# Keys and values of the attention branch: norm, rotation, high/low splits and transposes moved from the first pass to the convolution pass

## The chip, the cores and the metric

The kernel runs on one core of one Trainium2 chip. The metric is the device time of one execution in microseconds (us); lower is better. TensorE is written PE here (PEld for its weight loads), VectorE is DVE, ScalarE is ACT, GpSimd is POOL, and SP is the queue that issues most of the DMAs.

## The reference, cut to what matters

One layer of a hybrid backbone: 2048 latent tokens and 256 context tokens of width 1024 are normalised and modulated, projected by one matrix, mixed by two branches, and projected back. The change touches keys and values of branch B only:

```python
h = _rmsnorm(x, norm_w) * (1.0 + scale[:, None]) + shift[:, None]
hc = _rmsnorm(ctx, norm_w) * (1.0 + scale_c) + shift_c
qkv_c, beta_c, decay_c, kb_c, vb_c = _split_cols(hc @ w_state, STATE_SIZES)
kb_c = _rmsnorm(kb_c.reshape(b, lc, ATT_KV_HEADS, ATT_HD), k_norm_w)
qkv, beta_r, decay_r, kb, vb = _split_cols(h @ w_state, STATE_SIZES)
qa, ka, va, g, bt = _gdn_inputs(qkv, beta_r, decay_r, conv_w, a_log, dt_bias)   # 5-tap convolutions
kb = _axial_rope(_rmsnorm(kb.reshape(b, l, ATT_KV_HEADS, ATT_HD), k_norm_w), pos_row, pos_col)
vb = vb.reshape(b, l, ATT_KV_HEADS, ATT_HD)
ob = _latent_attention(qb, kb, vb, kb_c, vb_c, sink)
```

There are two key/value heads of 64, so per token 128 key numbers and 128 value numbers. Keys get a root-mean-square norm per head and, for latent tokens, a rotation by position; values stay as projected.

## The kernel before

Tokens are cut into 18 chunks of 128 (2 of context, then 16 latent). fp32 operands of the large products are split into a high and a low part (fp32r), so each product is three matmuls.

**First pass.** Chunks go in pairs: one context pair, then eight latent pairs (the loop over `gi`). For each pair: `load_x` (L280) brings two tiles `xt` of 512 KB; `norm_x` takes the mean square (half on ACT, L289, half on DVE, L292), the power -0.5 on POOL (`rsq`, L72), and scales `xt` (L295); `make_h` transposes 16 blocks on PE (L336), modulates on ACT (L337), and splits into `hh` on POOL (L339) and `hl` on DVE (L340); `tm_dense` multiplies 272 columns of `w_in` (decay and beta, keys, values) in 48 matmuls per pair (L366 to L368) into the PSUM tile `tmps`. Then `state_pair` reads `tmps`: it copies 16 columns to `bg` (L423), splits values into `vst` on ACT and DVE (L425, L426) and writes them to DRAM (`Vsp`), squares keys (L427), reduces them (L430, L431), takes the power on POOL (L72, tile `ssn`), scales (L435), rotates (L450 and L454 on DVE, L453 on POOL, with the table `cw` loaded and multiplied by the norm's weight at L443, L444), splits into `kh` (L456 to L458), transposes 4 blocks per chunk on PE (L464, tile `kt`), copies them out of PSUM (L465) and writes them to DRAM (`Ksp`). All of this works from one buffer each (`VB, SB, KB = 1, 1, 1`); `xt` has four.

**Convolution pass (`qkv`).** Twelve column tiles of 128 of the other branch's queries, keys and values are computed over five segments (one of 256 context tokens, four of 512 latent tokens) by `fm_dense` (L524 to L526, tile `lps`), copied out by ACT (L634), convolved (`conv`: L561 on ACT, four times L563 on DVE, L564 on ACT, L565 on DVE), and finished (`finish`): transposes (L595, tile `zt`), for keys also products `gps` (L604) times a decay loaded as `dtl` (L606) and another transposition (L618). The order of column tiles is `ORDER = [8, 9, 10, 11, 4, 5, 6, 7]`: four for values ("v part"), then four for keys ("k part"); the four for queries come later beside attention's own queries ("q part", `q_pass`). After each segment the loop calls `next(beside)`, which runs one step of a generator with other work; before the change this generator is `all_decays`, with 18 steps. There are 8 x 5 = 40 such calls in the v and k parts.

Later stages (gates, triangular solves, the recurrent scan, attention, projections) read `Ksp` and `Vsp` only from 1329 us on.

**What sets the order.** Each engine works through its instructions in a fixed order. This order is made when the kernel is built: the framework goes through the program by priority (the program's order) and places each instruction by a timeline that it estimates, so that work written later can be put ahead of work that waits. Tiles come from pools with a number of buffers; a tile that has no free buffer waits for the release of an older one. DMAs on SP are issued in order too: one that waits holds up those behind it.

Of the kernel before, what the change touches and what calls it, by code (L numbers as in the profile page):

```python
# [25 lines left out]
VB, SB, KB = 1, 1, 1  # L26
# [14 lines left out]
def _hybrid(ctx, tc, nc, V, S, G, T, ins, out, dbg, upto):  # L41
# [48 lines left out]
    Vsp = dscr("Vsp", [NC, 128, 2, 128])  # L90
    Qsp = dscr("Qsp", [NB, 128, 8, 128])
# [160 lines left out]
    if True:  # L252
        px_ = tc.tile_pool(name="p0x", bufs=4, reuse_waits="tile")
# [133 lines left out]
        wn = norm_w(pa, "k_norm_w")  # L387

# [29 lines left out]
        def state_pair(c, pss):  # L418

            vst = pa.tile([128, 2, 2, 2, 64], F32R, name="vst", bufs=VB)  # L420
            sq = pa.tile([128, 4, 64], F32, name="sq", bufs=SB)
            for i, ps in enumerate(pss):
                S.copy(bg[:, c + i], ps[:, 0:16])  # L423
                pv = ps[:, 144:272].rearrange("p (h d) -> p h d", d=64)
                S.copy(vst[:, i, :, 0], pv)  # L425
                V.tensor_tensor(vst[:, i, :, 1], pv, f32(vst[:, i, :, 0]), op=ALU.subtract)  # L426
                S.activation(sq[:, i * 2:i * 2 + 2], ps[:, 16:144].rearrange("p (h d) -> p h d", d=64), AF.Square)  # L427
            dma(Vsp[c:c + 2].rearrange("c p h x -> p c (h x)"), f32(vst.rearrange("p c h x d -> p c (h x d)")))
            ss = pa.tile([128, 4], F32, name="ssn")
            V.tensor_reduce(ss, sq, axis=AX.X, op=ALU.add)  # L430
            V.tensor_scalar(ss, ss, 1.0 / 64, EPS, op0=ALU.mult, op1=ALU.add)  # L431
            rsq(ss, ss)
            xn = pa.tile([128, 4, 64], F32, name="xn", bufs=SB)
            for i, ps in enumerate(pss):
                V.tensor_tensor(xn[:, i * 2:i * 2 + 2], ps[:, 16:144].rearrange("p (h d) -> p h d", d=64),  # L435
                                ss[:, i * 2:i * 2 + 2].unsqueeze(2).to_broadcast([128, 2, 64]), op=ALU.mult)
            y = xn
            if c < NCB:
                V.tensor_tensor(y, xn, wn[:, 0].unsqueeze(1).to_broadcast([128, 4, 64]), op=ALU.mult)
            else:  # L440
                cw = pa.tile([128, 2, 2, 64], F32, name="cw")
                with tc.issue_after(wm_dma.ins):
                    dma(cw, ins["k_rope"][(c - NCB) * 128:(c - NCB + 2) * 128].rearrange("(c p) x d -> p c x d", p=128))  # L443
                G.tensor_tensor(cw, cw, wn.unsqueeze(1).to_broadcast([128, 2, 2, 64]), op=ALU.mult)  # L444
# [15 lines left out]
            for i in range(2):  # L460
                kt = psum("hps" if c == NC - 2 and i else "kt", [128, 2, 2, 128], F32R, name="kt")
                for h in range(2):
                    for x in range(2):
                        T.transpose(kt[:, h, x], kh[:, i * 2 + h, x].rearrange("p r d -> p (r d)"), identr)  # L464
# [915 lines left out]
```

## Time and profile before

| | us |
|---|---|
| median of 3 runs | 2011.59 |
| lowest and highest run | 2009.54, 2018.15 |
| the profiled execution | 2010.84 |
| its span in the trace | 2009.1 |
| PE busy | 1936.4 (96% of the span) |
| DVE busy | 1407.5 (70%) |
| ACT busy | 786.1 (39%) |
| POOL busy | 654.0 (33%) |

The profiled execution took 0.75 us less than the median. Its time minus its span is 1.7 us. "Busy" of PE counts a matmul from its start to its modelled end, and successive matmuls overlap, so PE can be called busy while it delivers less than it could; therefore the distance from the start of one matmul to the next is read from the timeline, too. Times in the trace are counted from the span's start.

### The profile page before, as it was taken

Reading aid. Unit: us, or ns where it says so; the run is one execution under the profiler, and the core shown is the slowest. Engines: PE = TensorE matmul, PEld = TensorE weight load, DVE = VectorE, ACT = ScalarE, POOL = GpSimd, SP = SyncE. Lnnn points to the kernel's source line nnn. Section 1 sums busy time; section 2 is a strip of 40 time slices with the busy share of each in tenths; the row PEclk is TensorE's granted clock in tenths of the full one; section 3 lists DMA queues with packets and bytes.
Section 4 is the critical chain, followed back from the end, with each engine's and each line's share of the span. In section 5 each row is a group of like instructions: output and inputs, shape, how many; then the busy total and the mean of one; then the engine's idle time right before and its main releaser. Section 6 shows DMA issues by size and latency. Waiting matters only on the chain. (4 is left out here: it accounts for less than half of the span.)

```text
span 2009.1 us, 32070 instructions
## 1 busy us (share of the span) xinstructions
PE 1936.4 (96%) x11043; PEld 1625.3 (81%) x11043; DVE 1407.5 (70%) x2780; ACT 786.1 (39%) x1975; POOL 654.0 (33%) x751
## 2 busy tenths in 40 slices
PE   6999999989999999999999999999999999999999
PEld 3888888778998778877888888888778887878887
DVE  7979766667776899999777776536687878643322
ACT  5755545544443322211222233225665656531100
POOL 1752111225443212004222234323555444432221
PEclk8999999999999999999999999999999999999999
DMA  7552326764546633537887777674455555365542
GB/s 260 166 137 83 102 87 157 184 162 147 167 142 164 184 115 110 142 100 215 230 245 221 235 207 217 195 218 129 150 184 166 184 162 178 90 195 181 183 141 94
DMA packets 375511, 333.11 MB, mean 166 GB/s; under 512 B 83833, under 2 KB 299185, under 8 KB 374709
## 3 DMA queue, kind: packets, MB, share of 16 engines
q1 hardware_dynamic: 347924, 288.59, 49.7%
q10 hardware_dynamic: 27424, 42.48, 5.9%
q8 instruction: 87, 1.43, 0.3%
q14 instruction: 76, 0.61, 0.1%
HBM read 220.28 MB, written 109.13 MB: 164 GB/s over the span
## 5 line engine op out<-in xcount | busy, mean ns | idle before, releaser
L524 PE MATMUL rps<-hh,wh 128*128 128x512 f32 x768 | 308.4, 402 | 5.4 <-DVE rt L818 4.2
L526 PE MATMUL rps<-hh,wl 128*128 128x512 f32 x768 | 308.3, 402 | 0.0
L525 PE MATMUL rps<-hl,wh 128*128 128x512 f32 x768 | 306.4, 399 | 0.0
L563 DVE SCALAR_TENSOR_TENSOR cacc<-y,cw,cacc 128x512 f32<-128x512 f32 (+1 forms) x224 | 162.8, 748 | 22.4 <-ACT cacc L561 18.2
L524 PEld LDWEIGHTS rps<-hh,wh 128*128 128x128 f32 x768 | 145.0, 189 | 40.1 <-DVE rt L818 4.8
L524 PE MATMUL lps<-hh,wh 128*128 128x512 f32 (+1 forms) x448 | 171.4, 383 | 0.2 <-ACT y L634 0.2
L526 PE MATMUL lps<-hh,wl 128*128 128x512 f32 (+1 forms) x448 | 171.5, 383 | 0.0
L526 PEld LDWEIGHTS rps<-hh,wl 128*128 128x128 f32 x768 | 145.0, 189 | 32.6
L525 PE MATMUL lps<-hl,wh 128*128 128x512 f32 (+1 forms) x448 | 171.2, 382 | 0.0
L525 PEld LDWEIGHTS rps<-hl,wh 128*128 128x128 f32 x768 | 145.0, 189 | 32.4
L945 DVE TENSOR_TENSOR pl<-pt,ph 128x512 fp32r<-128x512 f32 x156 | 105.5, 686 | 42.1 <-ACT ph L943 41.2
L943 ACT CAST ph<-pt 128x512 fp32r<-128x512 f32 x156 | 90.1, 584 | 110.2 <-PE pt L941 77.2
L917 DVE CUSTOM_DVE_ANT_0 pr<-sc,band,sk 128x640 f32<-128x640 f32 (+1 forms) x128 | 106.8, 862 | 32.7 <-PE sc L913 16.9
L816 ACT ACTIVATE rt<-rps 128x512 f32<-128x512 f32 x96 | 57.2, 595 | 176.0 <-PE rps L526 159.1
L749 DVE TENSOR_TENSOR N<-N,btmp 128x62 f32<-128x62 f32 (+30 forms) x124 | 117.7, 949 | 3.0
L747 DVE TENSOR_TENSOR btmp<-N 128x62 f32<-128x62 f32 (+30 forms) x124 | 116.1, 936 | 3.1
L927 POOL TENSOR_SCALAR pr<-pr,sm 128x640 f32<-128x640 f32 (+1 forms) x128 | 99.2, 794 | 56.1 <-DVE sm L925 38.3
L1229 PE MATMUL pps<-yh,wph 128*128 128x512 f32 x256 | 105.2, 415 | 7.2 <-ACT yh L1211 5.0
L919 ACT ACTIVATE pr<-pr,sm 128x640 f32<-128x640 f32 (+1 forms) x128 | 104.0, 815 | 19.8 <-DVE sm L917 19.8
L246 DVE TENSOR_TENSOR wl<-wr,wh 128x512 fp32r<-128x512 f32 x120 | 91.6, 776 | 23.9 <-POOL wh L245 21.3
L245 POOL TENSOR_SCALAR wh<-wr 128x512 fp32r<-128x512 f32 x72 | 48.1, 683 | 167.1 <-PE lps L525 67.6
L1230 PE MATMUL pps<-yl,wph 128*128 128x512 f32 x256 | 101.7, 397 | 0.0
(301 smaller groups left out, 4922.8 us busy)
## 6 DMA issues: line engine op xcount, KB each, us to landing
wr<-in_w_in_dram SPq DMA_DIRECT2D x120, 256.0 KB
kw<-Ksp SPq DMA_DIRECT2D x28, 384.0 KB
x<-vsp SPq DMA_DIRECT2D x36, 256.0 KB
k<-ksp SPq DMA_DIRECT2D x34, 256.0 KB
kT<-kTsp SPq DMA_DIRECT2D x34, 256.0 KB
wm<-in_w_mod_dram SPq DMA_DIRECT2D x16, 512.0 KB
xt<-in_x_dram SPq DMA_DIRECT2D x16, 512.0 KB
dtl<-Dsp SPq DMA_DIRECT2D x32, 256.0 KB
```

The source lines that it names most:

```text
L524: T.matmul(ps, lhsT=wh[:, k], rhs=xh[:, k], start=k == 0, stop=False)
L525: T.matmul(ps, lhsT=wh[:, k], rhs=xl[:, k], start=False, stop=False)
L526: T.matmul(ps, lhsT=wl[:, k], rhs=xh[:, k], start=False, stop=k == kt - 1)
L563: V.scalar_tensor_tensor(a, y[:, t:t + n], cw[:, m, t:t + 1], a, op0=ALU.mult, op1=ALU.add)
L747: V.tensor_tensor(tv, A[:, m + 1:, m].unsqueeze(2).to_broadcast([h1 + n, r, m]), A[:, m, 0:m].unsqueeze(1).to_broadcast([h1 + n, r, m]), o ...
L749: V.tensor_tensor(A[:, m + 1:, 0:m], A[:, m + 1:, 0:m], tv, op=ALU.add)
L917: V.tensor_tensor_reduce(s_, ps[:, o:768], band[:, b0:b0 + W + 256], -0.125, sk[:, 1, hd:hd + 1], ALU.add, ALU.min, sm[:, h, 1:2])
L919: S.activation(s_, s_, AF.Exp, scale=-1.0, bias=sm[:, h, 1:2], accum_out=sm[:, h, 2:3])
L927: G.tensor_scalar(p[:, h, :W + 256], p[:, h, :W + 256], sm[:, h, 3:4], 1.0, op0=ALU.mult, op1=ALU.mult)
L945: V.tensor_tensor(pl, pt, f32(ph), op=ALU.subtract)
L1229: T.matmul(ps, lhsT=wh[:, k, ms], rhs=hs[k], start=k == 0, stop=False)
L1230: T.matmul(ps, lhsT=wh[:, k, ms], rhs=ls[k], start=False, stop=False)
```

## The change

`state_pair` now only copies `bg` and the 256 raw key and value columns out of PSUM (two ACT copies per chunk) and writes them as they are to a new DRAM tensor `Rsp`, 256 KB per pair. A new generator `key_pair` loads them again and does what `state_pair` did, with the same arithmetic: split of values, norm, rotation, split of keys, transposes, and writes of `Vsp` and `Ksp`. It takes its tiles from a pool `keys` with one buffer each, which lies where the decays' pool lay, and from the convolution pass's tags `st`, `o` and (in PSUM) `zt`, which it shares with `finish` and the decays. It is chained behind the 18 steps of the decays, and yields twice per pair: 18 + 18 = 36 steps of the 40 calls. `xt` gets six buffers instead of four.

```diff
-VB, SB, KB = 1, 1, 1
...
+    Rsp = dscr("Rsp", [NC, 128, 256])
...
-        px_ = tc.tile_pool(name="p0x", bufs=4, reuse_waits="tile")
+        px_ = tc.tile_pool(name="p0x", bufs=6, reuse_waits="tile")
...
         def state_pair(c, pss):
+            raw = pa.tile([128, 2, 256], F32, name="raw")
             for i, ps in enumerate(pss):
                 S.copy(bg[:, c + i], ps[:, 0:16])
...
+                S.copy(raw[:, i], ps[:, 16:272])
+            dma(Rsp[c:c + 2].rearrange("c p x -> p c x"), raw)
+
+        def key_pair(pool, c, wn):
+
+            raw = pool.tile([128, 2, 256], F32, name="raw")
+            dma(raw, Rsp[c:c + 2].rearrange("c p x -> p c x"))
+            cw = pool.tile([128, 2, 2, 64], F32, name="kcw")
+            if c >= NCB:
+                dma(cw, ins["k_rope"][(c - NCB) * 128:(c - NCB + 2) * 128].rearrange("(c p) x d -> p c x d", p=128))
+                G.tensor_tensor(cw, cw, wn.unsqueeze(1).to_broadcast([128, 2, 2, 64]), op=ALU.mult)
+            pv = raw[:, :, 128:256].rearrange("p c (h d) -> p c h d", d=64)
+            vst = pb.tile([128, 2, 2, 2, 64], F32R, name="vst", tag="st")
+            S.copy(vst[:, :, :, 0], pv)
+            V.tensor_tensor(vst[:, :, :, 1], pv, f32(vst[:, :, :, 0]), op=ALU.subtract)
+            dma(Vsp[c:c + 2].rearrange("c p h x -> p c (h x)"), f32(vst.rearrange("p c h x d -> p c (h x d)")))
...
+            S.activation(sq, xk, AF.Square)
...
+            V.tensor_reduce(ss, sq.rearrange("p c h d -> p (c h) d"), axis=AX.X, op=ALU.add)
+            V.tensor_scalar(ss, ss, 1.0 / 64, EPS, op0=ALU.mult, op1=ALU.add)
             rsq(ss, ss)
+            V.tensor_tensor(xk, xk, ss.rearrange("p (c h) -> p c h", c=2).unsqueeze(3).to_broadcast([128, 2, 2, 64]),
+                            op=ALU.mult)
+            yield
...
+                        V.tensor_tensor(halves(t2)[:, :, :, b], halves(xk)[:, :, :, 1 - b],
+                                        sw[:, :, b].unsqueeze(1).to_broadcast([128, 2, 2, 16]), op=ALU.mult)
+                G.tensor_tensor(xk, xk, cw[:, :, 0].unsqueeze(2).to_broadcast([128, 2, 2, 64]), op=ALU.mult)
+                V.tensor_tensor(xk, xk, t2, op=ALU.add)
             for i in range(2):
+                kh = pb.tile([128, 2, 2, 2, 64], F32R, name="kh", tag="st")
+                S.copy(kh[:, :, 0], xk[:, i].unsqueeze(2).to_broadcast([128, 2, 2, 64]))
+                V.tensor_tensor(kh[:, :, 1, 0], xk[:, i], f32(kh[:, :, 0, 0]), op=ALU.subtract)
+                V.tensor_copy(kh[:, :, 1, 1], f32(kh[:, :, 1, 0]))
+                kt = psum("zt", [128, 2, 2, 128], F32R, name="kt")
                 for h in range(2):
                     for x in range(2):
+                        T.transpose(kt[:, h, x], kh[:, h, x].rearrange("p r d -> p (r d)"), identr)
+                ks = pb.tile([128, 2, 2, 128], F32, name="ks", tag="o")
+                S.copy(ks, f32(kt))
+                dma(Ksp[:, :, :, (c + i) * 128:(c + i + 1) * 128].rearrange("h x p t -> p h x t"), ks)
+            yield
...
-    def all_decays():
+    def beside_kv():
...
+        dc_.__exit__(None, None, None)
+        with tc.tile_pool(name="keys", bufs=1, side="right", reuse_waits="tile") as kp:
+            wn = norm_w(kp, "k_norm_w")
+            for c in range(0, NC, 2):
+                for _ in key_pair(kp, c, wn):
+                    yield
...
-    qkv(ORDER, None, first_w, all_decays())
+    jobs = beside_kv()
+    qkv(ORDER, None, first_w, jobs)
+    for _ in jobs:
+        pass
     scalars2(pb)
```

More of the change, by code (lines that the diff above doesn't have):

```diff
@@ L385, in norm_w @@
             return wn
-        wn = norm_w(pa, "k_norm_w")
         def qk_norm_rope(pool, bufs, ps, nh, c, wn):
@@ L428, in state_pair @@
-            dma(Vsp[c:c + 2].rearrange("c p h x -> p c (h x)"), f32(vst.rearrange("p c h x d -> p c (h x d)")))
-            ss = pa.tile([128, 4], F32, name="ssn")
-            V.tensor_reduce(ss, sq, axis=AX.X, op=ALU.add)
+                S.copy(raw[:, i], ps[:, 16:272])
[11 more added lines that the diff above has]
+            V.tensor_tensor(vst[:, :, :, 1], pv, f32(vst[:, :, :, 0]), op=ALU.subtract)
+            dma(Vsp[c:c + 2].rearrange("c p h x -> p c (h x)"), f32(vst.rearrange("p c h x d -> p c (h x d)")))
+            xk = raw[:, :, 0:128].rearrange("p c (h d) -> p c h d", d=64)
+            sq = pool.tile([128, 2, 2, 64], F32, name="sq", tag="sq")
+            S.activation(sq, xk, AF.Square)
+            ss = pool.tile([128, 4], F32, name="ssn")
+            V.tensor_reduce(ss, sq.rearrange("p c h d -> p (c h) d"), axis=AX.X, op=ALU.add)
@@ L456, in state_pair @@
-            S.copy(kh[:, :, 0], y.unsqueeze(2).to_broadcast([128, 4, 2, 64]))
-            V.tensor_tensor(kh[:, :, 1, 0], y, f32(kh[:, :, 0, 0]), op=ALU.subtract)
-            V.tensor_copy(kh[:, :, 1, 1], f32(kh[:, :, 1, 0]))
-            ks = pa.tile([128, 2, 2, 2, 128], F32, name="ks", bufs=KB)
-            for i in range(2):
-                kt = psum("hps" if c == NC - 2 and i else "kt", [128, 2, 2, 128], F32R, name="kt")
+                        V.tensor_tensor(halves(t2)[:, :, :, b], halves(xk)[:, :, :, 1 - b],
+                                        sw[:, :, b].unsqueeze(1).to_broadcast([128, 2, 2, 16]), op=ALU.mult)
@@ L462, in state_pair @@
                 for h in range(2):
                     for x in range(2):
-                        T.transpose(kt[:, h, x], kh[:, i * 2 + h, x].rearrange("p r d -> p (r d)"), identr)
-                S.copy(ks[:, :, :, i], f32(kt))
-            for h in range(2):
-                dma(Ksp[h, :, :, c * 128:(c + 2) * 128].rearrange("x p t -> p x t"), ks[:, h].rearrange("p x c t -> p x (c t)"))
+                        T.transpose(kt[:, h, x], kh[:, h, x].rearrange("p r d -> p (r d)"), identr)
+                ks = pb.tile([128, 2, 2, 128], F32, name="ks", tag="o")
```

36 lines of the change are left out of this document (7 added, 29 removed).

## The prediction

> **What bounds the kernel now.** First the page:
>
> ```profile
> span 2009.1 us, 32070 instructions
> PE 1936.4 (96%) x11043; PEld 1625.3 (81%) x11043; DVE 1407.5 (70%) x2780; ACT 786.1 (39%) x1975; POOL 654.0 (33%) x751
> ```
>
> PE is the bound, so the change can gain only where PE falls short of its rate, and pays wherever PE gets work it cannot overlap. Next the windows over the stages that the change touches: start, first pass, v part, k part, start of the q part, rest of the q part (windows overlap; PEclk is the granted clock):
>
> ```profile
> core 0: us, PE busy (x) PEld busy (x) DVE busy (x) ACT busy (x) POOL busy (x), PEclk, DMA share, GB/s
> 0.00:50.00 50.00, 34.69 (x135) 16.99 (x136) 35.09 (x62) 29.70 (x47) 8.46 (x16) 0.83 0.74 261
> 50.00:140.00 90.00, 82.11 (x617) 76.84 (x616) 76.59 (x195) 60.26 (x168) 57.92 (x69) 0.96 0.48 153
> 160.00:200.00 40.00, 39.34 (x192) 32.25 (x191) 37.73 (x66) 24.51 (x59) 11.81 (x11) 1.00 0.25 79
> 253.00:375.00 122.00, 121.05 (x662) 102.00 (x661) 76.42 (x147) 62.00 (x183) 15.99 (x17) 1.00 0.50 131
> 350.00:460.00 110.00, 97.75 (x595) 83.66 (x594) 74.83 (x154) 54.76 (x182) 29.25 (x33) 0.97 0.67 173
> 475.00:600.00 125.00, 125.00 (x876) 114.38 (x876) 91.03 (x214) 55.56 (x168) 62.31 (x73) 1.00 0.48 144
> ```
>
> In the first pass PE idles 7.9 of 90 us and DVE is 85% busy; in the k part PE is full and DVE has 45.6 us free. PE loses more in the first pass than its idle time says. ACT's copies of `bg`, in the timeline, mark the ends of the context pair, the first latent pair and the last:
>
> ```profile
> 54.62 0.17 ACT L423 COPY bg<-tmps 128x16 f32<-128x16 f32 x1
> ...
> 63.33 0.17 ACT L423 COPY bg<-tmps 128x16 f32<-128x16 f32 x1
> ...
> 137.70 0.17 ACT L423 COPY bg<-tmps 128x16 f32<-128x16 f32 x1
> ```
>
> Eight latent pairs take 83.1 us, 10.4 each; the first took 8.7. What PE needs, by its timeline:
>
> ```profile
> 50.54 0.49 PE L336 MATMUL hps<-ident,xt 128*128 128x128 f32 x3
> 50.78 0.50 PE L366 MATMUL tmps<-wh,hh 128*128 128x272 f32 x2
> 51.12 0.49 PE L336 MATMUL hps<-ident,xt 128*128 128x128 f32 x3
> 51.37 0.37 PE L367 MATMUL tmps<-wh,hl 128*128 128x272 f32 x1
> 51.58 0.28 PE L368 MATMUL tmps<-wl,hh 128*128 128x272 f32 x1
> ...
> 52.57 0.28 PE L367 MATMUL tmps<-wh,hl 128*128 128x272 f32 x1
> ```
>
> Eight starts from 51.58 to 52.57 give 0.124 us per product. From 50.54 to 51.58 there are three products (0.37) and six transposes, 0.11 each. A pair's 48 products and 16 transposes cost 6.0 + 1.8 = 7.8 us. That is the floor without key transposes.
>
> **The change, part by part.** *Off the first pass.* DVE's rows of `state_pair`, 50 to 140 us, and PE's key transposes:
>
> ```profile
> L450 DVE TENSOR_TENSOR t<-xn,cw 128x64 f32<-128x64 f32 x28 | 6.0, 262 | 0.0
> L454 DVE TENSOR_TENSOR xn<-xn,t 128x256 f32<-128x256 f32 x7 | 5.4, 772 | 2.2 <-POOL xn L453 2.2
> L426 DVE TENSOR_TENSOR vst<-tmps,vst 128x128 fp32r<-128x128 f32 x18 | 5.0, 281 | 1.4 <-ACT vst L425 1.4
> L457 DVE TENSOR_TENSOR kh<-xn,kh 128x256 fp32r<-128x256 f32 x8 | 4.4, 548 | 0.9 <-ACT kh L456 0.8
> L435 DVE TENSOR_TENSOR xn<-tmps,ssn 128x128 f32<-128x128 f32 x16 | 3.9, 285 | 4.2 <-POOL ssn L72 4.1
> L430 DVE TENSOR_REDUCE ssn<-sq 128x4 f32<-128x256 f32 x8 | 3.3, 412 | 0.6 <-ACT sq L427 0.5
> L458 DVE CAST kh<-kh 128x256 fp32r<-128x256 f32 x8 | 2.6, 321 | 0.0
> L431 DVE TENSOR_SCALAR ssn<-ssn 128x4 f32<-128x4 f32 x8 | 1.7, 217 | 0.1
> L464 PE MATMUL kt<-identr,kh 128*128 128x128 f32 x57 | 8.6, 253 | 2.9 <-DVE kh L458 2.0 <-ACT ks L465 0.9
> ```
>
> DVE's eight rows sum to 32.3 us for about eight pairs, 4.0 each; without them DVE needs some 45 of the window's 90, and PE with 7.8 per pair is left the slowest. In DVE's queue of the first pass the middle of a pair was:
>
> ```order
> L435 TENSOR_TENSOR xn<-tmps,ssn 128x128 x2
> L292 SCALAR_TENSOR_TENSOR junk_1100,ss<-xt 128x512
> L450 TENSOR_TENSOR t_731<-xn,cw 128x4x16 x2
> L295 TENSOR_SCALAR xt<-xt,rstd 128x1024
> L450 TENSOR_TENSOR t_731<-xn,cw 128x4x16 x2
> ```
>
> and now, at the same place, is (L340 is the low part `hl`, which PE waits for; `h` is what ACT modulated):
>
> ```order
> L340 TENSOR_TENSOR hl_152<-h_836,hh_151 128x2x256
> L340 TENSOR_TENSOR hl_152<-h_847,hh_151 128x2x256
> L340 TENSOR_TENSOR hl_152<-h_858,hh_151 128x2x256
> L292 SCALAR_TENSOR_TENSOR junk_1175,ss<-xt 128x512
> L340 TENSOR_TENSOR hl_152<-h_947,hh_151 128x2x256
> ```
>
> Nothing but the next pairs' norms stands between the low parts now; the waits for POOL (4.1 us before L435, 2.2 before L454) are gone from ahead of PE's operands. What is late next is PE itself, or ACT, which modulates; ACT's own part gets shorter too (two copies per chunk remain). The pace lies between 7.8 (floor) and 10.4 (nothing gained); nearest is the first latent pair's 8.7, which still had DVE's key work beside it. I take 8.2: 8 x (10.4 - 8.2) = **-17.6 us** (-20.8 at the floor, -13.6 at 8.7).
>
> *Start.* SP issued before:
>
> ```order
> L280 DMA xt<-in_x_dram 128x1024 x2
> L443 DMA cw<-in_k_rope_dram 128x2x128 x2
> L357 DMA wr<-in_w_in_dram 128x272 x5
> L280 DMA xt<-in_x_dram 128x1024 x3
> L428 DMA Vsp<-vst 128x2x256
> ```
>
> and issues now:
>
> ```order
> L280 DMA xt<-in_x_dram 128x1024 x4
> L357 DMA wr<-in_w_in_dram 128x272 x5
> L280 DMA xt<-in_x_dram 128x1024 x2
> L422 DMA Rsp<-raw 128x2x256
> L280 DMA xt<-in_x_dram 128x1024 x2
> ```
>
> Two tiles of 512 KB more and two of 128 KB less stand ahead of the five weight loads that the first pair needs: 0.77 MB at 261 GB/s, 3 us at most, nothing if ACT's casts come last anyway; **+1.5**. Later `xt` loads stand behind `Rsp`, which waits for ACT's copy; with six buffers two pairs are loaded ahead, some 16 us of cover. Without that cover PE would wait a load per pair.
>
> *Into the k part, PE.* A key transpose among 512-wide products:
>
> ```profile
> 153.01 0.39 PE L524 MATMUL lps<-hh,wh 128*128 128x512 f32 x1
> 153.24 0.64 PE L464 MATMUL kt<-identr,kh 128*128 128x128 f32 x6
> 153.72 0.47 PE L525 MATMUL lps<-hl,wh 128*128 128x512 f32 x1
> 154.03 0.40 PE L526 MATMUL lps<-hh,wl 128*128 128x512 f32 x1
> ```
>
> From 153.01 to 154.03 are two products (0.23 each) and six transposes: 0.09 each. 57 of the 72 fell before 140 us, in the first pass; PE now does them where it is full: **+5.2**, with nothing to hide them.
>
> *Into the k part, the rest.* POOL's rows of the first pass, and DVE's of the k part (253 to 375 us):
>
> ```profile
> L72 POOL TENSOR_TENSOR ssn<-ssn,expo 128x4 f32<-128x4 f32 x8 | 10.1, 1259 | 4.2 <-DVE ssn L431 4.1
> L453 POOL TENSOR_TENSOR xn<-xn,cw 128x256 f32<-128x256 f32 x7 | 6.6, 941 | 6.3 <-DVE t L450 6.3
> L444 POOL TENSOR_TENSOR cw<-cw,wn 128x256 f32<-128x256 f32 x6 | 5.6, 926 | 4.0 <-DMA cw<-in_k_rope_dram 4.0
> ```
> ```profile
> L563 DVE SCALAR_TENSOR_TENSOR cacc<-y,cw,cacc 128x512 f32<-128x512 f32 (+1 forms) x66 | 46.3, 719 | 14.3 <-ACT cacc L561 13.2
> L606 DVE TENSOR_TENSOR p<-gps,dtl 128x512 f32<-128x512 f32 (+1 forms) x11 | 6.8, 619 | 15.8 <-DMA dtl<-Dsp 14.2 <-PE gps L604 1.5
> L204 DVE TENSOR_TENSOR gm<-glo,mats 128x512 fp32r<-128x512 f32 x2 | 2.9, 1454 | 1.7 <-PE dps L206 1.7
> L204 DVE TENSOR_TENSOR gm<-ghi,mats 128x512 fp32r<-128x512 f32 x3 | 2.0, 679 | 0.0
> ```
>
> DVE had in the middle of the k part only the convolution's steps (L563, L565), the products with the decays (L606) and the seams between segments:
>
> ```order
> L606 TENSOR_TENSOR p<-gps,dtl 128x512
> L636 MEMSET y 128x2
> L563 SCALAR_TENSOR_TENSOR cacc<-y,cw,cacc 128x512 x4
> L565 SCALAR_TENSOR_TENSOR cacc<-y,cacc 128x512
> L638 COPY y<-y 128x2
> L606 TENSOR_TENSOR p<-gps,dtl 128x512
> ```
>
> Now the key work of a pair of chunks stands between them (L567 and L610 are the old L563 and L606; `raw`, `kcw`, `t` are the new generator's tiles):
>
> ```order
> L610 TENSOR_TENSOR p<-gps,dtl 128x512
> L444 TENSOR_TENSOR raw<-raw,ssn 128x2x128
> L567 SCALAR_TENSOR_TENSOR cacc<-y,cw,cacc 128x512
> L455 TENSOR_TENSOR t_3268<-raw,kcw 128x4x16 x4
> L435 TENSOR_TENSOR vst<-raw,vst 128x4x64
> L567 SCALAR_TENSOR_TENSOR cacc<-y,cw,cacc 128x512
> L458 TENSOR_TENSOR raw<-raw,t_3268 128x2x128
> ```
>
> The four steps of one convolution no longer stand together. L444 waits for POOL's power and L458 for POOL's product; behind them on DVE queue convolution steps, and for these wait ACT's L564 and PE's transposes `zt`. On PE a `kt` that comes late holds up the products behind it. `kt` also takes 18 turns of the three `zt` buffers, beside 20 of the convolutions. DVE gets 9 x 4.0 = 36: 76.4 + 36 = 112 of 122 + 5, 88%. ACT, with 60 of 122 us free there, gets seven operations per pair and none that waits for PE except the copies of `kt`; I cost it at nothing, and if its cover went it would show as DVE waiting for `kh`. PE stayed full with DVE at 73% and a like chain beside it (475 to 600), and lost 0.7 of 40 us at 94% (160 to 200); the first pass, at 85%, lost 9%. So between 0 and 9% of 127, 0 to 11 us; I take **+3**, nearer the convolution rows. SP gets some 45 DMAs more, by their shapes 10 MB over 122 us, 85 GB/s on top of 131. A load of `raw` has one buffer and waits for the pair before it; behind it on SP stand the loads of `dtl`, for which L606 waits already. Both lie in the same bound. So does the start of the q part (12 us of PE idle), whose queue is unchanged but for its first blocks.
>
> *A rule against it.* In the last two rows above the same 512-wide DVE product took 679 ns alone and 1454 where POOL's own was beside it: 0.8 us lost per POOL operation of that size. The Trainium skill's "SBUF — State Buffer" (§ SBUF: two separate sides) says DVE and GpSimd hold a shared port pair exclusively, also for DVE operations with two SBUF inputs, as the convolution's are; by it the sum would lose most of its gain. By rows: POOL gets 9 x 1.26 + 8 x (0.94 + 0.93) = 26 us there; at full price DVE needs 138 of 127, +11 instead of +3, sum 0. I don't take it: L72 handles four numbers per partition, and the rows of 475 to 600 hold POOL 62 us beside a full PE.
>
> **Sum.** -17.6 + 1.5 + 5.2 + 3 = -7.9. The profiled execution took 2010.84 (span 2009.1), so 2002.9; the median of before was 0.75 higher: 2003.7.
>
> **The rivals.** (1) *PE reaches its floor, nothing is lost later:* -20.8 + 5.2 = -15.6, 1996. For: DVE, ACT and POOL all fall well below PE. Against: the pass starts cold (clock 0.83). 0.2. (2) *The pass was bound by the chain load, norm, transpose, split rather than DVE's load,* pace 9.6: -6.4 + 9.7 = +3.3, 2015. For: DVE was idle 13 of 90. Against: six buffers lengthen the lead. 0.2. (3) *Slower: DVE becomes the k part's bound.* With POOL's 26 blocking it and half of its 30.1 us of waits (L563, L606) staying: 76.4 + 36 + 26 + 15 = 153 instead of 122, +31; -16.1 + 31 = +15, 2027. It decides from a k part longer by 26 us on (16.1 + 10). Against: 160 to 200, where DVE at 94% cost PE 0.7 us. 0.1. The page's rule above is what would feed this one. That the work stays outside is excluded: 36 steps fit in 40 calls. My forecast has 0.5.
>
> **Numbers.** Changes within 0.5% (10 us) cannot be told from none. Below 2001.5 lie rival 1 and two fifths of the forecast's spread (1998 to 2009): 0.40. Slower takes rival 3 and a little of rival 2's tail: 0.11. Range 1995 to 2017: it leaves out rival 3 and the ends of 1 and 2.
>
> **What would show it.** Right: `bg` copies of latent pairs 8.2 us apart, the last near 122; clock 1.00 from 50 us on; k part 8 us longer, DVE near 88%. Wrong: pairs still 10 apart; or PE waiting on `kh`, `zt` or `gps` in the k part for over 11 us.

## The result, and the profile after

The change made the kernel slower: the median of nine runs is 2022.51 us (2019.66 to 2027.41), that of the kernel before in the same measurement 2009.94 us; the ratio on record is 1.0056, with a 95% interval from 1.0044 to 1.0067 (the medians alone give 1.0063). The forecast was 2003.7 us, 6 us faster; its range ended at 2017. The profiled execution took 2019.8 us. One slow execution, of 3836.5 us in the run with three key tiles in one ring, is left out of all that follows. The page of the changed kernel:

```profile
span 2018.1 us, 32167 instructions
PE 1932.6 (96%) x11043; PEld 1623.9 (80%) x11043; DVE 1408.3 (70%) x2780; ACT 793.2 (39%) x1984; POOL 659.6 (33%) x751
```

The span is 9.0 us longer, with as many matmuls as before. First the first pass. ACT's copies of `bg` in the timeline, as in the prediction (end of the context pair, of the first latent pair, of the last):

```profile
54.63 0.17 ACT L420 COPY bg<-tmps 128x16 f32<-128x16 f32 x1 [0.18 <-PE tmps L368]
...
63.78 0.16 ACT L420 COPY bg<-tmps 128x16 f32<-128x16 f32 x1
...
120.26 0.17 ACT L420 COPY bg<-tmps 128x16 f32<-128x16 f32 x1 [0.17 <-PE tmps L368]
```

Eight latent pairs take 65.6 us, 8.2 each; before they took 83.1. The gain that the change was to bring is there in full. The windows of the changed kernel, the same stages as in the prediction, show where it went:

```profile
core 0: us, PE busy (x) PEld busy (x) DVE busy (x) ACT busy (x) POOL busy (x), PEclk, DMA share, GB/s
50.00:125.00 75.00, 72.37 (x573) 70.45 (x572) 50.20 (x89) 47.06 (x127) 35.90 (x47) 1.00 0.42 118
235.00:300.00 65.00, 65.00 (x337) 54.17 (x336) 42.86 (x100) 33.81 (x88) 12.82 (x15) 1.00 0.42 123
300.00:430.00 130.00, 105.57 (x590) 89.11 (x588) 88.38 (x213) 71.18 (x216) 34.67 (x35) 0.88 0.73 195
475.00:600.00 125.00, 123.53 (x859) 112.64 (x858) 92.91 (x216) 56.54 (x168) 60.10 (x69) 1.00 0.51 154
```

The first pass runs at full clock with DVE at 67%, where it was 85%; PE is full from 235 to 300 us and nearly so again from 475 us. Between 300 and 430 us, which is most of the k part and the start of the q part, PE stands for 24 of 130 us and its clock is at 0.88. DVE is busy for 88.4 of these 130 us, 68%: less than the 73% at which the prediction had seen PE full.

A finer measure is used below for every run. The same product of PE is looked up in two traces, and its start in the kernel before is taken from its start in the other: a negative number is a lead. The changed kernel has a lead of 18.8 us at 286 us (in the time of the kernel before), and is 10.2 us late at 490: it loses 29.0 us between. After that it stays 9 to 11 us late to the end. The same work, in the kernel before and in the changed one:

```profile
319.00:460.00 141.00, 128.75 (x773) 110.32 (x772) 94.07 (x192) 70.54 (x231) 34.39 (x37) 0.98 0.67 172
```
```profile
300.00:471.00 171.00, 144.17 (x859) 123.61 (x858) 120.34 (x285) 93.51 (x294) 54.86 (x56) 0.91 0.74 197
```

141 us have become 171. PE's idle time went from 12.3 to 26.8 us, 14.6 more. Its busy time grew by 15.4 us: 5.2 by the prediction's figure for the transposes, most of the rest by the clock. What PE waits for in the changed kernel, 250 to 430 us (columns: operand waited for, us in all, times, longest):

```profile
PE gps L622 <- DVE p L610: 12.3, 5, 4.2
PE kt L467 <- ACT kh L461: 6.1, 2, 4.7
PE zt L599 <- DVE cacc L569: 3.6, 1, 3.6
```

Few, long waits, where there had been next to none up to 400 us (3.3 us in all from 250 to 400). The clock fell to half three times between 300 and 430 us. The windows cut there (the column before the DMA share is the granted clock):

```profile
300.00:312.70 12.70, 9.48 (x70) 8.27 (x68) 11.13 (x21) 7.13 (x20) 2.48 (x4) 1.00 0.70 170
312.70:319.50 6.80, 5.94 (x17) 4.93 (x18) 3.28 (x13) 5.05 (x19) 1.69 (x2) 0.50 1.02 305
...
353.70:357.10 3.40, 3.25 (x15) 2.98 (x16) 2.08 (x4) 1.98 (x4) 0.33 (x1) 0.51 0.82 222
...
401.50:422.00 20.50, 9.83 (x45) 8.99 (x46) 13.87 (x34) 9.72 (x29) 8.76 (x7) 0.50 0.65 167
```

PE stood from 309.9 to 313.6 us, from 350.4 to 353.8, from 399.7 to 403.9, from 407.1 to 409.9 and from 411.9 to 416.6. In the 30.7 us at half clock it worked for 19.0 us, which at full clock are 9.5: the five stalls, 18.8 us together, cost half as much again. The Trainium skill's "TensorE: Matmul & The Clock Gate" (Part 1) has such a rule, that the clock falls to half after an idle window of some 3.4 us. The trace agrees in the lengths, 3.4, 6.8 and 20.5 us, multiples of that window. It does not agree that the whole window has to be idle: the clock fell 2.7, 3.3 and 1.7 us after PE's last product, and at 1524.4 us it fell though PE had been busy for 1.3 of the 3.4 us before. The measurement decides here.

Last, SP, whose rows no table of busy time holds. Its timeline in the changed kernel ahead of the stall at 350 us:

```profile
343.87 0.61 SPq L582 DMA_DIRECT2D offsp<-p  x1
344.52 0.60 SPq L574 DMA_DIRECT2D dtl<-Dsp  x1
345.22 0.47 SPq L427 DMA_DIRECT2D raw<-Rsp  x1
345.73 0.47 SPq L596 DMA_DIRECT2D kTsp<-cacc  x1
347.31 0.37 SPq L704 DMA_DIRECT2D wrq<-in_w_in_dram  x1
347.78 1.25 SPq L581 DMA_DIRECT2D Nsp<-pt  x2
349.07 0.61 SPq L582 DMA_DIRECT2D offsp<-pt  x1
349.78 0.55 SPq L470 DMA_DIRECT2D Ksp<-ks  x1
350.43 0.47 SPq L704 DMA_DIRECT2D wrq<-in_w_in_dram  x1
```

SP issues one transfer after the other with short gaps (the longest 1.1 us), about half a microsecond for each, and the key work's (`raw`, `Ksp`) stand between the k part's own. From the first write of `ksp` to the last of `offsp` SP issued 190 transfers in 141.2 us before, 111.3 us of issuing or 79%; now it is 233 in 173.1 us, 132.6 us or 77%. So SP is no busier; the stretch got longer at the same density.

Two of the stalls can be followed back to a transfer (ACT and DVE ahead of 350 us, SP and ACT ahead of 416 us):

```profile
348.30 0.42 ACT L439 ACTIVATE sq<-raw 128x256 f32<-128x256 f32 x1 [1.55 <-DMA raw<-Rsp]
348.75 0.42 DVE L441 TENSOR_REDUCE ssn<-sq 128x4 f32<-128x256 f32 x1 [0.87 <-ACT sq L439]
...
413.72 0.60 SPq L436 DMA_DIRECT2D Vsp<-vst  x1
...
416.14 0.41 ACT L461 CAST kh<-raw 128x256 fp32r<-128x256 f32 x1 [1.93 <-DMA Vsp<-vst]
```

At 348 us ACT waits for `raw` to land, DVE for ACT, and the product `p`, for which PE waits, comes behind them in DVE's order, at 352.99. At 416 us `kh` waits until `Vsp` is written: DVE had finished `vst` at 405.6, but SP came to its write only at 413.7, having issued other transfers for 6.8 us of the time between.

### The profile page after: what moved, and what is told of

Its sections match the earlier page's. It is cut to its first block, busy times and chain, and to the rows that moved or that the text cites. A ratio compares the mean times of both kernels' runs of the same rounds, so it can differ in the third digit from the quotient of the medians.

```text
span 2018.1 us, 32167 instructions
## 1 busy us (share of the span) xinstructions
PE 1932.6 (96%) x11043; PEld 1623.9 (80%) x11043; DVE 1408.3 (70%) x2780; ACT 793.2 (39%) x1984; POOL 659.6 (33%) x751
## 5 line engine op out<-in xcount | busy, mean ns | idle before, releaser
L567 DVE SCALAR_TENSOR_TENSOR cacc<-y,cw,cacc 128x512 f32<-128x512 f32 (+1 forms) x224 | 162.2, 746 | 18.8 <-ACT cacc L565 16.6
L528 PE MATMUL lps<-hh,wh 128*128 128x512 f32 (+1 forms) x448 | 173.1, 387 | 0.8 <-ACT y L638 0.7
L530 PEld LDWEIGHTS rps<-hh,wl 128*128 128x128 f32 x768 | 144.4, 188 | 31.9
L930 ACT ACTIVATE pr<-pr,sm 128x640 f32<-128x640 f32 (+1 forms) x128 | 104.0, 815 | 19.3 <-DVE sm L928 19.2
L1242 PE MATMUL pps<-yh,wpl 128*128 128x512 f32 x256 | 101.7, 397 | 0.0
```

Source lines behind the costliest of these rows:

```text
L528: T.matmul(ps, lhsT=wh[:, k], rhs=xh[:, k], start=k == 0, stop=False)
L530: T.matmul(ps, lhsT=wl[:, k], rhs=xh[:, k], start=False, stop=k == kt - 1)
L567: V.scalar_tensor_tensor(a, y[:, t:t + n], cw[:, m, t:t + 1], a, op0=ALU.mult, op1=ALU.add)
L930: S.activation(s_, s_, AF.Exp, scale=-1.0, bias=sm[:, h, 1:2], accum_out=sm[:, h, 2:3])
L1242: T.matmul(ps, lhsT=wl[:, k, ms], rhs=hs[k], start=False, stop=k == 3)
```

## The experiments

Each run is compared with the kernel before on the same chip. "Lost" is the difference of the leads at 286 and at 490 us, from its trace; the changed kernel's is 29.0 us.

### First round: rings, queues, prefetch

A ring is the set of buffers that the tiles of one tag take in turn. Theory A: the shared rings `st` and `o`. Theory B: SP's queue and the landing of transfers. Theory C: the chain of waits itself in the fixed queues. The first edit gave two of the key tiles an idle ring:

```diff
-            vst = pb.tile([128, 2, 2, 2, 64], F32R, name="vst", tag="st")
+            vst = ev.tile([128, 2, 2, 2, 64], F32R, name="vst", tag="rt")
...
-                kh = pb.tile([128, 2, 2, 2, 64], F32R, name="kh", tag="st")
+                kh = ev.tile([128, 2, 2, 2, 64], F32R, name="kh", tag="rt")
```

> The changed kernel gained 18.9 us in the first pass and lost 30.3 us from there to the q part, of which 5.2 are the moved transposes. Here the key work's tiles vst and kh take turns in the two idle buffers of tag rt instead of the two buffers of tag st, which it shared with the spills of the convolutions; ks stays in tag o. Theory A (shared rings: each turn lasts until a DMA has landed, so spills and key work hold each other up in ACT's queue): more than half of the 25 us goes, 2005 to 2009. Theory B (SP's queue and the landing of its DMAs are late): no change, 2017 to 2023. Theory C (the chain of waits itself between ACT, DVE, POOL and PE in fixed queues): 2014 to 2020.

Measured: 2019.28 us, ratio 1.0058 (1.0039 to 1.0078), lost 29.4. With `ks` in that ring too:

```diff
-                ks = pb.tile([128, 2, 2, 128], F32, name="ks", tag="o")
+                ks = ev.tile([128, 2, 2, 128], F32, name="ks", tag="rt")
```

> As with vst and kh in the two buffers of tag rt, and ks there too, so that tags st and o are the convolutions' alone; three kinds of key tiles now share two buffers. Theory A (shared rings): the best of the four, 2000 to 2007, since ACT's copies pt no longer wait for Ksp<-ks either. Theory B (SP's queue): 2017 to 2023. Theory C (chain of waits): 2014 to 2022, the key chain being slower by itself.

Measured: 2032.53 us, 1.0132 (1.0084 to 1.0179), lost 41.2: three tiles in one ring of two are worse. Theory A falls. The writes of the key work issued by ACT instead of SP:

```diff
-            dma(Vsp[c:c + 2]...
+            adma(Vsp[c:c + 2]...
...
-                dma(Ksp[:, :, :, ...
+                adma(Ksp[:, :, :, ...
```

> The writes of Vsp and Ksp (27 of the 45 moved DMAs) are issued from ACT's queue instead of SP's; tiles as in the changed kernel. Theory A (shared rings): small, 2015 to 2023, since each turn still lasts until the write has landed. Theory B (SP's queue): at least a third of the 25 us goes, 2005 to 2012. Theory C (chain of waits): no gain or slower, 2019 to 2026, as ACT also has to issue.

Measured: 2021.92 us, 1.0071 (1.0051 to 1.009), lost 30.5. SP issues 207 transfers in its stretch of 173.9 us (ACT 24) and is down to 68%, and nothing is won. The DMA share of the run's windows is what it was (0.75 in the changed kernel, too):

```profile
300.00:350.00 50.00, 41.62 (x256) 35.56 (x254) 35.06 (x82) 28.07 (x86) 14.70 (x14) 1.00 0.75 202
```

I took theory B to have fallen with this. That was too early: only its half, the order in SP's queue, had been tried. The Trainium skill's "DMA: Bandwidth & Descriptors" (§ Issuing engines are not separate DMA queues) says that transfers issued by several engines run on the same 16 DMA engines, so that only issue time is saved; the 0.75 agrees.

The buffers of `xt` back to four, the rest as changed:

```diff
-        px_ = tc.tile_pool(name="p0x", bufs=6, reuse_waits="tile")
+        px_ = tc.tile_pool(name="p0x", bufs=4, reuse_waits="tile")
```

> The changed kernel with four xt buffers, as before, instead of six. If the first pass gained by the work taken off DVE: its last products still end 12 to 18 us earlier than before, and the time is 2018 to 2024. If it gained by the longer prefetch: they end less than 8 us earlier, and the time is 2028 to 2034.

Measured: 2029.41 us, 1.0112 (1.0075 to 1.0149). The lead is 17.8 us at 144 us (18.2 with six) and 16.1 at 286; lost 34.1. So the first pass's gain comes from the work taken off, not from the longer lead of the loads. The time itself fell where the other theory had put it (2028 to 2034), because this run lost 5 us more than the changed kernel between 286 and 490 us, for a reason that was not followed up.

### Second round: parts of the key work left out or moved

C1: PE's transposes queued behind fresh splits. C2: DVE's queue, with the norm and rotation ahead of `p` and the convolution. C3: POOL as a slow partner. No transposes:

```diff
-                kt = psum("zt", [128, 2, 2, 128], F32R, name="kt")
...
-                dma(Ksp[...], ks)
+                dma(Ksp[...], f32(kh.rearrange("p h x r d -> p h x (r d)")))
```

> The key work without its transposes: the split keys go to DRAM straight from the split tile (the same bytes, so the layout of the keys is not the reference's), and ACT's copy of the transposed keys falls away with them. Theory C1 (PE stands because its 57 key transposes sit in its fixed queue right behind the splits that feed them, and hold a bank of the zt ring): the whole later loss of some 30 us goes, with 5.2 us of the transposes' own time in it; about 19 us faster than the kernel before (ratio near 0.991) and PE's waits for p, kh and cacc near nothing between 250 and 425 us. Theory C2 (DVE's fixed queue: the product p and the convolutions stand behind the norm and rotation of the keys, which themselves wait for POOL and DMA): only the 5.2 us and a little of ACT's time go; still 4 to 7 us slower than the kernel before (ratio 1.002 to 1.0035), with PE's waits for p left.

Measured: 2023.52 us, 1.0066 (1.0044 to 1.0088), lost 30.4. PE's waits in this run, 130 to 500 us:

```profile
PE zt L594 <- DVE cacc L564: 16.7, 7, 4.1
PE gps L617 <- DVE p L605: 11.6, 5, 6.1
```

The waits for `kh` are gone, and others took their place; not even the 5.2 us of the transposes came back. C1 falls, with one reserve: the write now reads `kh` itself, which so holds its buffer of the shared ring until the write has landed. No norm and rotation (the lines from `kcw` and `sq` to the last `V.tensor_tensor(xk, xk, t2...)` taken out):

> The key work without norm and rotation (square, sum, power, products, the table's load and its POOL product left out); splits, transposes and their writes stay. Theory C2: the wait for p goes and with it the idle time and the half clock, some 25 of the 30 us lost later; about 14 us faster than the kernel before (ratio near 0.993). Theory C1: PE's transposes and their waits stay; the time is that of the changed kernel less 3 us at most (ratio 1.004 to 1.006).

Measured: 2020.02 us, 1.0048 (1.0032 to 1.0064), lost 28.7:

```profile
PE gps L598 <- DVE p L586: 11.5, 5, 4.4
PE zt L575 <- DVE cacc L545: 8.2, 5, 3.9
```

The wait for `p` is about as long as in the changed kernel (12.3), though the work that was to stand ahead of it is gone. C2 falls. This run also has the eight loads of the rotation's table fewer, and loses as much. POOL's two products on DVE:

```diff
-                G.tensor_tensor(cw, cw, wn...
+                V.tensor_tensor(cw, cw, wn...
...
-                G.tensor_tensor(xk, xk, cw[:, :, 0]...
+                V.tensor_tensor(xk, xk, cw[:, :, 0]...
```

> The two products that POOL does for the keys are done by DVE instead (POOL keeps the power). Theory C3 (POOL as a slow partner in the chain, or POOL and DVE holding each other up at their port): the chain of each pair is shorter by two crossings and by POOL's slow products; 5 to 15 us faster than the changed kernel (ratio 0.998 to 1.003). Theories C1 and C2: no gain, DVE has a few us more in its queue; ratio 1.005 to 1.008.

Measured: 2025.51 us, 1.0093 (1.0061 to 1.0124), lost 34.3. C3 falls. Transposes one step after their splits:

```diff
+            late_kt()     # at the start of a pair: transposes, copy and write of the pair before
...
-                kh = pb.tile([128, 2, 2, 2, 64], F32R, name="kh", tag="st")
+                kh = ev.tile([128, 2, 2, 2, 64], F32R, name="kh", tag="rt")
```

> The splits of a pair of keys are put into the idle ring of the values' stage (two buffers of 2 KB), and the transposes with their copy and write are issued one step later, ahead of the next pair's work, so that PE and ACT find them ready. The same instructions as the changed kernel has. Theory C1 (PE waits for fresh splits in its queue): the waits for kh go and most of the loss but the 5.2 us of transposes; 10 to 14 us faster than the kernel before (ratio 0.993 to 0.995). Theory C2: PE still waits for p behind DVE's key work; within 4 us of the changed kernel (ratio 1.0035 to 1.0075).

Measured: 2018.64 us, 1.0042 (1.0028 to 1.0057), lost 25.8. A little at most: the interval overlaps that of the changed kernel.

After this round two things were in all the runs that lost: the transfers, and steps on ACT and DVE whose place the scheduler chose.

### Third round: the transfers alone, and another place

Theory D: the transfers. Transfers of the same shapes in the kernel before, without any key work:

```diff
+        for c in range(0, NC, 2):        # behind the decays' steps
+            tr = ev.tile([128, 2, 256], F32, name="tr", tag="rt")
+            dma(tr, ins["x"][...])
+            yield
+            dma(Vd[...], tr)
+            for i in range(2):
+                dma(Kd[...], tr...)
+            yield
```

> The kernel before, with nothing but transfers added at the steps where the changed kernel does its key work: per pair of chunks 256 KB read from x into the idle ring rt, and a step later 256 KB written in the pattern of the values' splits and two times 256 KB in the pattern of the transposed keys, to tensors that nobody reads; the kernel's own work is untouched. Theory D (what is lost in the k part is room on the DMA engines, which stand at shares of 0.56 to 0.81 there before the change, whatever the engines compute): 9 x 1.0 MB more at some 200 to 250 GB/s is 38 to 47 us of all DMA engines, and the kernel gets 12 to 25 us slower (ratio 1.006 to 1.0125), with DMA shares over 0.75 between 270 and 450 us. Theory C (the compute steps in the fixed queues): under 4 us slower (ratio below 1.002).

Measured: 2022.65 us, 1.0081 (1.0062 to 1.0099). But this is no test of the k part: nothing makes these transfers wait, so the scheduler put them early, and SP issued them from 147 to 223 us. The kernel is 14.4 us late at 205 us, and loses nothing more (14.6 at 490). It shows that such transfers cost PE time in the v part, too, whose DMA share was 0.25 (160 to 200 us); ACT waited there for 28.7 us until writes of `vsp` had landed (140 to 230 us), before for 6.1. The smaller one, `tr[0:16]` in place of `tr`:

> The same transfers as in the run beside it, as many and at the same steps, but of 16 of the 128 partitions: an eighth of the bytes. Theory D (bytes and packets on the DMA engines): 0 to 3 us slower than the kernel before (ratio 1.000 to 1.0015). If it is the issues on SP and what queues behind them: about as slow as the run with the whole transfers.

Measured: 2017.42 us, 1.0052 (1.0033 to 1.0071); 6.6 us late at 205. An eighth of the bytes leaves less than half of the loss by the traces (6.6 of 14.4), two thirds by the medians (9 of 15 us). The key work beside the q part instead (`raw` in the ring `rt`, `kcw` in a ring of the queries' pool):

```diff
+    def q_and_keys(pool):
+        kk = keys(pool)
+        for _ in q_pass(pool):
+            next(kk)
+            yield
+        for _ in kk:
+            yield
...
-        jobs = q_pass(pq)
+        jobs = q_and_keys(pq)
```

> The changed kernel with the key work beside the q part (after 430 us) and no longer beside the k part: one step after each step of the queries' pass. Same work, other place; the DMA share there is 0.46 to 0.53 before. Theory D: the k part keeps its old time, the q part has room for the transfers; the first pass's 18.9 us stay, less 5.2 us of transposes and 2 to 6 us of waits: 8 to 13 us faster than the kernel before (ratio 0.9935 to 0.996). Theory C: the same steps in the same fixed queues, beside a part in which PE is 98% busy and DVE 72 to 77%: the loss of some 25 us moves with them; 4 to 12 us slower than the kernel before (ratio 1.002 to 1.006).

Measured: 2021.23 us, 1.0077 (1.0057 to 1.0097). Its windows over the k part:

```profile
300.00:350.00 50.00, 49.10 (x288) 42.14 (x287) 31.94 (x64) 26.07 (x86) 9.54 (x8) 1.00 0.65 158
350.00:400.00 50.00, 45.18 (x262) 37.31 (x261) 33.45 (x67) 24.28 (x81) 13.73 (x18) 1.00 0.72 185
```

With the key work gone the k part keeps the lead (19.1 us at 286, 16.9 at 447), so it was the key work that cost there and not the earlier start. But the q part then loses 18 us (1.3 late at 709), and the later stages 9 more (10.6 late at 1695), whose cause was not followed up. There was no room in the q part either. Values split in the first pass, as before; only keys go raw through DRAM:

```diff
+                S.copy(vst[:, i, :, 0], pv)                     # in state_pair, from PSUM
+                V.tensor_tensor(vst[:, i, :, 1], pv, f32(vst[:, i, :, 0]), op=ALU.subtract)
+            dma(Vsp[...], vst...)
...
-            raw = pool.tile([128, 2, 256], F32, name="raw")
+            raw = pool.tile([128, 2, 128], F32, name="raw")
```

> The values' part of the change undone: values are split from PSUM in the first pass and written there, as before; only the keys go raw through DRAM. In the k part a third of the transfers go (128 KB of raw and 256 KB of splits of 1,152 KB per pair), in the first pass DVE and ACT get some 1.5 us per pair back. Theory D: a third of the 25 us lost beside the transposes comes back, 8 us, less 3 to 6 us of the first pass's gain: 2 to 6 us faster than the changed kernel (ratio 1.0025 to 1.0045). Theory C: the k part loses only two short steps per pair; about the changed kernel's time or 2 to 6 us slower (ratio 1.0055 to 1.0085).

Measured: 2016.55 us, 1.0049 (1.0032 to 1.0065); a lead of 19.9 us at 286, lost 25.2. The values' part of the change gains nothing in the first pass, and its removal gives 4 us back in the k part, by one trace of each; the ratios' intervals overlap.

### Fourth round: transfers and compute apart, in the k part

Now with transfers that hang on the k part's own, by reading back what it has just written:

```diff
+    def traffic(h, c0):
+        tr = ev.tile([128, 2, 256], F32, name="tr", tag="rt")
+        dma(tr, kTsp[h, :, c0 * 128:c0 * 128 + 512].rearrange("p (c x) -> p c x", x=256))
+        dma(Vd[...], tr)
+        for i in range(2):
+            dma(Kd[...], tr...)
...
             dma(kTsp[h, :, c0 * 128:c0 * 128 + n], z)
+            if m < 7 and c0 > NCB:
+                traffic(h, c0)
```

> The kernel before with transfers alone in the k part: behind nine of its writes of the keys' columns 256 KB read back from them into the idle ring rt, and 256 KB and twice 256 KB written from there to tensors nobody reads, in the patterns of the values' splits and the transposed keys. The first pass is that of before. Theory D (transfers: the DMA engines' room and the landing of the k part's own spills): the loss of 20 to 25 us comes without any key work, ratio 1.008 to 1.0125. Theory E (the compute steps of the key work among the k part's own): under 4 us, ratio below 1.002.

Measured: 2033.12 us, 1.0127 (1.0108 to 1.0145), and 22.0 us lost between 286 and 490, in a kernel that does none of the key work there. PE's waits, 130 to 700 us:

```profile
PE gps L630 <- DVE p L618: 17.6, 8, 6.2
PE zt L607 <- DVE cacc L567: 6.2, 5, 3.4
```

PE's waits are those of the changed kernel, and DVE is less busy than there (30.0 us of 50 at most). One step behind PE the two differ. What `p` waits for on DVE, 260 to 440 us, here and in the changed kernel:

```profile
DVE p L618 <- DMA dtl<-Dsp: 23.5, 11, 6.5
```
```profile
DVE p L610 <- DMA dtl<-Dsp: 8.0, 7, 3.4
```

Here the long waits are for `dtl`, up to 6.5 us; in the changed kernel `p` also stands behind key steps that wait for others, as at 348 us. In the kernel before, `p` waited for `dtl` for 20.3 us, but never for more than 2.6 at a time. On SP the write of `tr` waits here for its read to land, too (4.2 us in six waits), as no transfer of the changed kernel does. This run's windows:

```profile
300.00:350.00 50.00, 49.68 (x275) 41.61 (x274) 26.81 (x51) 25.96 (x89) 4.67 (x4) 1.00 0.74 202
350.00:400.00 50.00, 43.51 (x229) 36.32 (x228) 30.03 (x55) 22.64 (x69) 9.48 (x12) 0.93 0.80 217
400.00:450.00 50.00, 39.85 (x245) 34.99 (x244) 27.90 (x60) 21.78 (x71) 11.62 (x11) 0.90 0.74 198
```

The counterpart has all the compute and none of the transfers in the k part (the first pass writes raw numbers to their places, three transfers per pair):

```diff
-            dma(raw, Rsp[c:c + 2].rearrange("c p x -> p c x"))
+            G.memset(raw, 1.0)
...
-            dma(Vsp[...], vst...)      # likewise kcw's load (a memset) and the writes of ks
```

> The changed kernel with all the key work's compute, on a tile that POOL fills with ones, and without its transfers in the k part: nothing is read from DRAM, and splits and keys are not written there (the first pass writes raw values to their places, three transfers a pair as before, so that later stages read what they read; what they read is not the reference's). Theory D: the k part loses the 5.2 us of transposes and up to 4 us; 9 to 14 us faster than the kernel before (ratio 0.993 to 0.9955). Theory E: the loss stays at 20 to 30 us; ratio 1.001 to 1.0056.

Measured: 2000.78 us, 0.9955 (0.9939 to 0.9972), lost 10.7, of which the transposes would be about half by the prediction's 5.2. Its profiled execution was the slowest of ten (2008.34). Its windows:

```profile
300.00:350.00 50.00, 48.25 (x293) 42.02 (x291) 38.34 (x98) 32.30 (x103) 18.40 (x22) 0.97 0.62 153
350.00:400.00 50.00, 41.78 (x231) 35.26 (x230) 35.85 (x91) 30.01 (x92) 15.41 (x18) 0.90 0.54 135
400.00:450.00 50.00, 44.60 (x306) 40.65 (x305) 38.00 (x82) 24.62 (x81) 21.20 (x23) 0.97 0.72 188
```

DVE is as busy here as in the changed kernel (112 of these 150 us, 106 there), and after 400 us PE is back at 44.6 of 50. Theory D stands in the main: the transfers alone cost 22.0 us, the compute alone 10.7. But SP's stretch is 161.0 us long in this run, with 194 issues, at 70%: 20 us longer than before with four issues more. Its length does not follow the number of issues alone.

The two edits of the earlier rounds that helped most, together (values split in the first pass, transposes a step later):

> The two edits with the best results together: values split and written in the first pass as before, keys' transposes one step after their splits, which lie in the ring rt. Each alone was some 2 us faster than the changed kernel (1.0049 and 1.0042 for 1.0056). Theory D: a third of the transfers is gone: 1.001 to 1.004. Theory E: the steps are fewer and none of PE's waits for a fresh split: 0.998 to 1.003.

Measured: 2012.81 us, 1.0025 (1.0006 to 1.0045), lost 21.7. It is the best version with all of the work, and still not faster than the kernel before. The key steps at a later priority:

```diff
+                    with tc.high_priority(-600):
+                        next(kk, None)
```

> The changed kernel with the key steps at a later priority (by 600), so that the scheduler puts the k part's own instructions ahead of them where both could go. Theory E (the place of the steps in the engines' fixed order): the waits for p and the convolutions shrink, 5 to 15 us faster than the changed kernel (ratio 0.998 to 1.003). Theory D: the same transfers in the same stretch; within 4 us of the changed kernel (ratio 1.0035 to 1.0075).

Measured: 2038.92 us, 1.0152 (1.0136 to 1.0168), lost 52.0. Both theories missed. The order does matter: PE now waits 13.9 us for `p` and 8.6 for ACT's copies `y` between 250 and 430 us. A better order was not found; it is only shown that the scheduler's own was not the worst.

### Fifth round: bytes or number

The transfers of the fourth round, as many, with 16 of the 128 partitions:

```diff
-        dma(Vd[c0:c0 + 2].rearrange("c p h x -> p c (h x)"), tr)
+        dma(Vd[c0:c0 + 2].rearrange("c p h x -> p c (h x)")[0:16], tr[0:16])
```

> The run with transfers alone in the k part, with as many transfers at the same places, but of 16 of the 128 partitions: an eighth of the bytes. If the price is the bytes and packets that the DMA engines have to move: 0 to 6 us slower than the kernel before (ratio 1.000 to 1.003). If it is SP's fixed queue (four issues more at nine places, and the wait of the write for its read's landing, behind which the k part's own issues stand): 15 to 25 us (ratio 1.0075 to 1.0125).

Measured: 2024.73 us, 1.0085 (1.007 to 1.01), lost 19.2. The windows have a DMA share at or below that of the kernel before (0.62, 0.73, 0.64 there):

```profile
300.00:350.00 50.00, 49.57 (x276) 41.68 (x275) 29.56 (x57) 26.18 (x86) 4.67 (x4) 1.00 0.57 144
350.00:400.00 50.00, 42.43 (x223) 35.42 (x221) 25.76 (x48) 20.48 (x66) 9.71 (x12) 0.93 0.61 154
400.00:450.00 50.00, 42.15 (x266) 36.76 (x266) 31.52 (x67) 26.04 (x79) 11.82 (x11) 0.97 0.63 155
```

An eighth of the bytes costs two thirds as much by the medians (16 of 25 us). By the traces it costs nearly all (19.2 of 22.0), but this trace is of the slowest of four executions and the other of the fastest. In the k part it is mainly the number of transfers, not their size. SP issued 228 in its stretch of 163.7 us, at 79% once more.

Last, fewer transfers and all of the work: values split in the first pass; the keys' splits, which lay twice on the partitions, stored once, with one write per pair, and read twice by attention:

```diff
-    Ksp = dscr("Ksp", [2, 2, 128, NC * 128])
+    Ksp = dscr("Ksp", [2, 2, 64, NC * 128])
...
+            dma(Ksp[:, :, :, c * 128:(c + 2) * 128].rearrange("h x p t -> (x p) h t"), ks...)
...
+                for r in range(2):
+                    dma(f32(kw[r * 64:r * 64 + 64, h, :, :W]), Ksp[h, :, :, t0:t0 + W]...)
```

> The changed kernel with fewer transfers in the k part, and all of the reference's work: values split and written in the first pass as before; the keys' splits stored once and no longer twice on the partitions (two transposes per chunk and no copy on DVE; one write of 256 KB per pair in rows of 1 KB in place of two writes of 256 KB in rows of 512 bytes), and attention reads them twice, by two transfers in place of one. In the k part 512 KB per pair are left of 1,152 KB, and three issues of six. If the transfers are the cause: of the first pass's 19 us stay all but 2.6 us of transposes and 0.45 x 20 = 9 us; 4 to 10 us faster than the kernel before (ratio 0.995 to 0.998), where attention hides its added issues. If the compute steps were the cause: 1.000 to 1.003, as the run with values first and late transposes gave 1.0025.

Measured: 2021.89 us, 1.0067 (1.0049 to 1.0086). In the k part the step helped: lost 19.0 in place of 29.0, 2.6 us late at 668 (of the five issues per pair, not six, three are left; half of the transposes are gone, too). But its lead at 286 is only 16.5 us, and the run is 12.6 us late at 1594, in attention, which has the added transfers; that they are the cause was not tested. No version that does all the work beat the kernel before.

## Why the prediction was wrong, point by point

- **First pass, -17.6: right.** 83.1 us became 65.6, -17.5, at the predicted pace of 8.2, with the clock at 1.00. It came from the work taken off; the six buffers, to which I gave "some 16 us of cover", were hardly needed for it (17.8 of 18.2 us with four). Rival 2, a pass bound by its chain, is out.
- **Start, +1.5:** the context pair ends at 54.63 us, before at 54.62: nothing.
- **Transposes, +5.2:** not to be seen by themselves. With them left out the stretch loses 30.4 us in place of 29.0. Where PE waits for others, a few us of its own work cost nothing, and taking them away gives nothing. The term belongs to a k part in which PE is the bound, and that k part was gone.
- **The rest of the k part, "+3, between 0 and 11": the step that failed.** Measured are 29.0 us in all, 24 beside the transposes. Two things were wrong in it. It took DVE's busy share as the measure of what PE would lose; DVE ended at 68%, and PE's idle time still grew by 14.6 us. And it priced the transfers by bytes ("some 45 DMAs more, by their shapes 10 MB over 122 us, 85 GB/s on top of 131") and put them into DVE's bound. Transfers alone cost the kernel before 22.0 us in this part, and with an eighth of the bytes still 19.2. There were 43 more of them, on a queue that was issuing for 79% of the time already. I had named the very place, the loads of `dtl` behind `raw` on SP, and had not counted SP's time.
- **What would show it wrong** was met: PE waited for `gps`, `kt` and `zt` for 22 us in the k part, where the sign was 11.
- **Half clock** was in no term: 9.5 us, since the stalls come in pieces of 2.8 to 4.8 us.
- **Rival 3** had the right side (2027) and the wrong mechanism; that its +31 us for the k part is near the measured 30 (141 us became 171) is luck. DVE was not the bound, and with POOL's products moved to DVE the kernel got no faster (1.0093 against 1.0056), as it should have if POOL had blocked DVE. The port rule that was weighed beside it found no support: DVE's 512-wide convolution steps took 789 ns in the mean between 300 and 450 us, before 753, which over 59 of them is 2 us. (One chance rests on a slip that changes nothing else: 2001.5 cuts off a third of 1998 to 2009, not two fifths.)

**What is shown and what is open.** Shown: the loss comes from the key work in the k part; with that work moved elsewhere the k part keeps its lead. Transfers alone cost 22.0 us there, the compute alone 10.7, and most of the transfers' price in this part hangs on their number. Open is how they cost it. In numbers of SP's issues the changed kernel fits: 43 more at 132.6 / 233 = 0.57 us are 24.5 us, at a density of 0.79 some 31 us of stretch (measured 31.9). The runs with fewer fit less and less: the 9 writes less of the run with values first would give 6.5 us and it got 4; the 18 less of the last run would give 13 and it got 10, both with less compute, too; the 8 less of the run without norm would give 6 and it got 0.3. And with 24 writes on ACT's queue and SP down to 68% nothing was won. Whether there ACT's issuing took the place of SP's, or the landing of each transfer and the rings that wait for it count beside the issue, was not separated. Nor does it add up: 22.0 and 10.7 are more than 29.0, and the order of the same steps alone took the loss from 29.0 to 52.0.

## What to carry to other kernels

Count a moved step's transfers on the queue that issues them, not only their bytes: a queue that issues for four fifths of a stage can hold up what stands in it, as it held the write of `Vsp` for 8 us here, and no table of engine busy times shows it. A stage in which PE is 100% busy can still lose by added steps, though every engine has time left; test such a cover by adding the suspected load alone to the kernel before. And look at the clock behind each stall: the five here cost half as much again.

## What the runs showed of the hardware that was not expected

Transfers cost PE time in a stage where the DMA engines were a quarter busy: 36 of them in the v part (share 0.25 before) made the kernel 14.4 us late, and with an eighth of the bytes still 6.6. An issue occupied SP for about half a microsecond at either size: the added ones of the fourth round took 0.41 to 0.60 us in the mean of their kinds, those with an eighth of the bytes 0.47 to 0.60. And the granted clock fell to 0.50 in single gaps of PE of 3.5 to 4.2 us, 1.7 to 3.3 us after its last product, and at 1524.4 us after 3.4 us in which PE was busy for 1.3.
